# Sums of down-projection weights: from SyncE's queue to ScalarE's, from one pair of buffers to two

## The chip, the cores and the metric

The kernel runs on one core of one Trainium2 chip, in one launch. The metric is the device time of an execution in microseconds, as the median of several runs. A core has TensorE (matrix products; PE in the profile, its weight loads PEld), VectorE (DVE), ScalarE (ACT), GpSimd (POOL) and SyncE (SP). Each engine takes its instructions in the order in which they were put on it. Here SyncE issues nearly all DMAs; ScalarE and GpSimd can issue some as well, and a DMA that has to wait for a semaphore then holds up what stands behind it on the engine that issues it.

## The reference

One post-norm layer of a streaming encoder, for a prompt of 2048 tokens and for 8 sequences of 16 tokens with stored states (together 17 tiles of 128 tokens), in float32. Cut to what matters:

```
z = x @ w_in                                   # 1024 -> 2824: q,k,v,o of 4 mLSTM heads, gates, 8 q and 2 kv attention heads
hm = sigmoid(om) * head_norm(mlstm_chunkwise(qm, km * 128**-0.5, vm, logi, logf, C0, n0, m0))
ha = band_attend(rope(qa), rope(ka), va, mask, sinks)   # softmax over the window and one learned sink per head:
     # mx = max(max(s), sink);  p = exp(s - mx) / (sum(exp(s - mx)) + exp(sink - mx))
h = layer_norm(alpha * x + concat(hm, ha) @ w_out)
u = h @ w_up                                   # 1024 -> 5632
c = b_conv + causal depthwise conv of width 3 over u
a, g = split(c)
y = layer_norm(alpha * h + (silu(g) * a) @ w_down)      # 2816 -> 1024
```

## The kernel before

Every product is made of three single-pass products of a high and a low part (`hi` is the operand rounded by ScalarE, `lo` the rest, taken by VectorE: `split`, L215). The large products are done with seven half-size products in place of eight (Strassen's scheme in Winograd's form), so sums and differences of blocks of the operands are needed. For the down projection these are sums of blocks of `w_down`, and they are the subject here.

**Stages.** `i_dense` (the input projection, 4 blocks of tokens, each with 5 groups `g` of output columns and 7 products `s`), then `o_block` (the output projection, 5 blocks), then `f_ups` (up projection and convolution) and `f_downs` (down projection). While the first two run, three generators (`t_sample`, `m_chain`, `a_chain`) weave the mLSTM and the attention of finished tokens between the dense products; the class `Chains` decides by estimated costs where each step is put.

**Order.** TensorE's instructions stay in the order in which the program makes them (`manual_schedule`, L236). Those of all other engines are put in order by the framework's scheduler, for which the order of the program is a priority; an instruction that it takes to be ready can go ahead of many that stand before it.

**The products.** In input blocks 1 to 3 the products go in this order, as (g, s): (0,1) (0,7) (0,6) (0,2), then for g = 0 to 3: [(g,6) (g,7) (g,2) for g > 0], (g,5) (g+1,1) (g,3) (g,4), and (4,6) (4,7) (4,5) (4,2) (4,3) (4,4) at the end. A product is 24 matmuls (L704) into one of three banks A, B, C (`self.ib`). `i_after` (L768) moves finished banks out: copies by ScalarE (L763, L771, L779, L799), additions by VectorE (L775, L777).

**The sums.** `d_sums(k, step)` (L840) makes the two sums of pair k of weight tiles, for k = 0 to 10. Step 0 loads two tiles of 128 x 1024 (512 KB each) from `wdn` into `x` and `y` (L844, L845); step 1 is four subtractions of halves on VectorE (L850 to L853); step 2 stores both into the DRAM tensor `zt` (L855, L856), from which the down projection reads much later. `x` and `y` take the buffers `xr1` and `xr3`, one of each, so pair k + 1 can be loaded only when pair k has been stored. In input blocks 2 and 3 step 0 is written behind product s = 6 of the groups 0 to 3, step 1 behind s = 5 and step 2 behind s = 3 (for group 3: behind 6, 2 and 5), which makes k = 0 to 7. The output projection makes k = 8 to 10, one in the first half of a block (L1606).

**Who else uses these buffers.** `xr1` to `xr4` hold the four quarters of an input block (`x_load`, L534; L537 is the DMA), which `x_steps` (L539) turns into the seven operands: steps `t1` to `t4` are sums of quarters, the others split one. In the output projection `x_pair` (L884) loads its operands into the same four and splits them (L896, L897).

**The sink.** For each tile of queries `scores` (L1291, twice per tile, 32 calls in all) makes a tile `sc` of masked scores. One more column of it is filled with the sinks (L1297, GpSimd), VectorE copies the masked scores and takes their maxima (L1307), L1310 makes the bias, and `exps` (L1313) takes the exponentials with their sum, sink column included, on ScalarE.

Of the kernel before, what the change touches and what calls it, by code (L numbers as in the profile page):

```python
# [8 lines left out]
F32 = mybir.dt.float32  # L9
# [5 lines left out]
P = 128  # L15
D = 1024
# [37 lines left out]
NK2 = NFF // 2  # L54
# [150 lines left out]
class Prog:  # L205
# [381 lines left out]
    def i_dense(self):  # L587
        nc, a = self.nc, self.a
# [33 lines left out]
        for item in self.items:  # L622
# [45 lines left out]
            if g == last and b + 1 < nb:  # L668
                if s == 7:
                    self.rope_load(IBLOCKS[b + 1][2], 2)  # L670
                for x in passages[b > 0].get(s, ()):
                    if x == "load":
                        self.spare = True
                        self.x_load(b + 1, 1, 2, 3, 4)
                    else:
                        self.x_steps(b + 1, x)
            if g == last and b + 1 == nb and s in (7, 5, 2, 3):
# [1 line left out]
            with self.tc.issue_after(behind) if behind and b == 0 else nullcontext():  # L679
                self.advance()  # L680

            if b >= nb // 2 and g < last:

                steps = (6, 2, 5) if g == last - 1 else (6, 5, 3)
                if s in steps:
                    self.d_sums(sums, steps.index(s))
                    sums += s == steps[2]
        self.sums = sums
        self.logs_of(nb - 1)
        self.chains.hold = False  # L690
# [149 lines left out]
    def d_sums(self, k, step):  # L840
        nc, V = self.nc, self.nc.vector
        if step == 0:
            self.txy = x, y = [self.xp.tile([P, D], F32, name="txy", tag=f"xr{q}", bufs=1) for q in (1, 3)]
            nc.sync.dma_start(x, self.a["wdn"][k])  # L844
            nc.sync.dma_start(y, self.a["wdn"][NK2 + k])  # L845
            return
        x, y = self.txy
        if step == 1:
            l, r = slice(0, 512), slice(512, D)
            V.tensor_sub(x[:, l], x[:, r], x[:, l])  # L850
            V.tensor_sub(x[:, r], y[:, r], x[:, r])
            V.tensor_sub(y[:, r], y[:, r], x[:, l])
            V.tensor_sub(y[:, l], y[:, l], y[:, r])  # L853
            return
        nc.sync.dma_start(self.zt[0, k], x)  # L855
        nc.sync.dma_start(self.zt[1, k], y)  # L856

    def rope(self, A, t, nt):

# [411 lines left out]
    def swa(self, t):  # L1271
# [19 lines left out]
        def scores(j0):  # L1291

            sink, nsink = [x.rearrange("p (k j) -> p k j", k=2)[:, :, j0:j0 + 2] for x in (self.sink, self.nsink)]
            sc = self.work("sc", [P, 4, 2 * P + 4], bufs=2)
            mx, sm = [self.work(n, [P, 4], bufs=2) for n in ("amx", "asm")]
            w = lambda x: x.rearrange("p (k j) -> p k j", k=2)
            nc.gpsimd.tensor_copy(sc[:, :, N:N + 1].rearrange("p (k j) o -> p k (j o)", k=2), sink)  # L1297
            ps = [self.bank([P, 2, 2, P], "psc") for _ in range(2)]
            for j in range(2):
                for i, (q, k) in enumerate(((qh, self.kh), (qh, self.kl), (ql, self.kh))):  # L1300
                    for kvh in range(2):
                        rs = slice(64 * kvh, 64 * kvh + 64)
                        nc.tensor.matmul(ps[kvh][:, j, :nk], q[rs, j0 + j], k[rs, sel], start=i == 0, stop=i == 2)  # L1303
            for kvh in range(2):
                for j in range(2):
                    c = 2 * kvh + j
                    V.tensor_tensor_reduce(out=sc[:, c, :N], in0=ps[kvh][:, j, :nk].rearrange("p a b -> p (a b)"), in1=mask, scale=1.0, scalar=-3e38,  # L1307
                                           op0=ALU.add, op1=ALU.max, accum_out=mx[:, c:c + 1])

            V.scalar_tensor_tensor(w(mx), w(mx), -0.125, nsink, op0=ALU.mult, op1=ALU.min)  # L1310
            return sc, mx, sm

        def exps(sc, mx, sm):  # L1313
# [872 lines left out]
```

## Time and profile before

| | |
|---|---|
| median of 3 runs | 2317.24 us (2315.28 to 2321.0) |
| profiled execution, its own time | 2316.15 us |
| its span | 2314.3 us |
| granted TensorE clock | 0.996 |
| busy TensorE / VectorE / ScalarE / GpSimd | 99% / 78% / 55% / 12% |
| DMA, mean over the span | 273 GB/s |

A busy time is a share of the whole span, an average over stages. TensorE's number says that it hardly ever stands; where it does is read from its waits. In the rows of the profile the names on both sides of `<-` are the tile written and the tiles read, `L` is the line of the kernel, and SPq and ACTq mark DMA issues of SyncE and ScalarE.

### The profile page before, as it was taken

How to read it: one execution, taken by the hardware profiler on the slowest of the kernel's cores; microseconds unless marked ns; L12 is line 12 of the kernel's file. 1: busy time of each engine (PE TensorE's matmuls, PEld its weight loads, DVE VectorE, ACT ScalarE, POOL GpSimd, SP SyncE). 2: the span in 40 equal slices, each digit the busy share in tenths (PEclk: the TensorE clock that was granted, in tenths of full speed). 3: DMA queues.
4: the chain of work that ended last, by engine and by line, in shares of the span. 5: the costliest groups of instructions: out<-in, count | busy, mean ns of one | idle time of the engine just before them, and what ended most of it. 6: DMA issues, size and time to landing. Idle time of an engine off the chain costs nothing.

```text
span 2314.3 us, 39788 instructions
## 1 busy us (share of the span) xinstructions
PE 2281.9 (99%) x14293; PEld 2094.9 (91%) x14293; DVE 1808.1 (78%) x3075; ACT 1269.0 (55%) x2377; POOL 279.5 (12%) x509
## 2 busy tenths in 40 slices
PE   8999999999999999999999999999999999999998
PEld 8999989989877778999999999999999978888876
DVE  8777687787688888998788777678766786895987
ACT  5453466776766655555656555555555544444442
POOL 0001000000011212121002000013111200100200
PEclk9999999999999999999999999999999999999999
DMA  7888999999977757888778889978898776756743
GB/s 276 287 308 297 301 309 336 314 310 342 315 269 240 240 201 270 303 319 311 276 289 274 306 304 311 315 264 287 312 294 261 225 282 208 261 175 215 255 157 108
DMA packets 300166, 632.38 MB, mean 273 GB/s; under 512 B 47869, under 2 KB 141121, under 8 KB 299969
## 3 DMA queue, kind: packets, MB, share of 16 engines
q1 hardware_dynamic: 295296, 616.14, 77.9%
q0 software_dynamic: 3520, 10.56, 1.4%
q10 hardware_dynamic: 1152, 3.15, 0.4%
q8 instruction: 113, 1.85, 0.3%
q14 instruction: 85, 0.69, 0.1%
HBM read 458.11 MB, written 171.64 MB: 272 GB/s over the span
## 4 chain that ended last, share of the span: by engine, by line
PE 76%; DVE 5%; DMA 4%; issue 2%; ACT 1%; SPq 0%; POOL 0%; DVEq 0%; ACTq 0%; POOLq 0%
PE dps L1873 19%; PE fup L1873 19%; PE dps L704 7%; PE dps L2083 6%; PE fht L2083 6%; PE fup L2083 6%; PE dps L222 2%; PE dps L224 2%; PE dps L223 2%; PE ppo L1348 1%; PE psc L1303 1%; PE ppt L1342 1%; DVE w L218 1%; PE fht L1697 1%; DMA txy<-wdn 0%
## 5 line engine op out<-in xcount | busy, mean ns | idle before, releaser
L1873 PE MATMUL dps<-hh,uw 128*128 128x384 f32 (+1 forms) x1848 | 478.7, 328 | 2.0 <-DVE u L1904 2.0
L1873 PE MATMUL fup<-hh,uw 128*128 128x384 f32 (+1 forms) x1848 | 478.2, 328 | 1.5 <-ACT ua L1894 1.5
L1873 PEld LDWEIGHTS dps<-hh,uw 128*128 128x128 f32 x1848 | 330.5, 188 | 2.2 <-DVE u L1904 2.2
L1873 PEld LDWEIGHTS fup<-hh,uw 128*128 128x128 f32 x1848 | 330.0, 188 | 2.0 <-ACT ua L1894 1.9
L1930 DVE SCALAR_TENSOR_TENSOR cc<-u,cw,cc 128x768 f32<-128x768 f32 (+1 forms) x264 | 258.1, 978 | 64.9 <-ACT cc L1928 55.5
L1873 PE MATMUL fup<-hl,uw 128*128 128x384 f32 (+1 forms) x924 | 302.5, 327 | 1.7 <-DVE hl L218 1.7
L1873 PE MATMUL dps<-hl,uw 128*128 128x384 f32 (+1 forms) x924 | 302.8, 328 | 0.0
L704 PE MATMUL dps<-w,oh 128*128 128x256 f32 x1344 | 254.3, 284 | 0.7 <-DVE zev L777 0.7
L217 ACT CAST uw<-wraw 128x1024 fp32r<-128x1024 f32 x126 | 123.0, 979 | 223.8 <-PE dps L2083 120.1
L218 DVE TENSOR_TENSOR w<-wraw,w 128x1024 fp32r<-128x1024 f32 (+2 forms) x167 | 189.4, 1141 | 56.1 <-ACT w L217 48.9
L217 ACT CAST w<-wraw 128x1024 fp32r<-128x1024 f32 (+2 forms) x167 | 163.0, 985 | 107.3 <-PE dps L704 38.9
L704 PEld LDWEIGHTS dps<-w,oh 128*128 128x128 f32 x1344 | 210.5, 188 | 11.8 <-issue 8.1
L218 DVE TENSOR_TENSOR uw<-wraw,uw 128x1024 fp32r<-128x1024 f32 x126 | 142.4, 1131 | 65.7 <-ACT uw L217 65.5
L704 PE MATMUL dps<-w,ol 128*128 128x256 f32 x672 | 187.8, 279 | 0.0
L704 PE MATMUL dps<-oh,w 128*128 128x256 f32 x896 | 170.9, 285 | 6.6 <-ACT mr L1153 3.8
L1873 PEld LDWEIGHTS fup<-hl,uw 128*128 128x128 f32 x924 | 173.5, 188 | 2.4 <-DVE hl L218 2.3
L2083 PE MATMUL fup<-uw,fu 128*128 128x512 f32 x726 | 174.2, 396 | 0.6 <-DVE uw L218 0.6
L1873 PEld LDWEIGHTS dps<-hl,uw 128*128 128x128 f32 x924 | 173.8, 188 | 0.0
L2083 PEld LDWEIGHTS fup<-uw,fu 128*128 128x128 f32 x726 | 136.6, 188 | 34.1 <-DVE uw L218 1.1
L2083 PE MATMUL dps<-uw,fu 128*128 128x512 f32 x660 | 165.3, 396 | 1.1 <-DVE uw L218 1.1
L1928 ACT ACTIVATE cc<-u,cw 128x768 f32<-128x768 f32 (+1 forms) x132 | 132.2, 1002 | 57.8 <-DVE u L1910 28.5
L704 PEld LDWEIGHTS dps<-oh,w 128*128 128x128 f32 x896 | 142.2, 191 | 13.1 <-ACT mr L1153 4.1
(318 smaller groups left out, 4567.0 us busy)
## 6 DMA issues: line engine op xcount, KB each, us to landing
uw<-zw SPq DMA_DIRECT2D x176, 512.0 KB, 5.1
zw<-uw SPq DMA_DIRECT2D x88, 512.0 KB, 3.7
w<-zws SPq DMA_DIRECT2D x72, 512.0 KB, 6.2
wv<-wup SPq DMA_DIRECT2D x66, 512.0 KB, 5.0
wraw<-wi SPq DMA_DIRECT2D x65, 512.0 KB, 5.1
wraw<-zt SPq DMA_DIRECT2D x60, 512.0 KB, 4.3
wraw<-wdn SPq DMA_DIRECT2D x45, 512.0 KB, 4.3
wraw<-wo SPq DMA_DIRECT2D x40, 512.0 KB, 4.5
```

The costliest lines, as they stand in the source:

```text
L217: nc.scalar.copy(hi, src)
L218: nc.vector.tensor_sub(lo, src, hi.bitcast(F32))
L222: mm(out, ah, bh, start=start, stop=False)
L223: mm(out, ah, bl, start=False, stop=False)
L224: mm(out, al, bh, start=False, stop=stop)
L704: mm(o, l, r, start=s in (1, 7) and c == k == i == 0, stop=k == 3 and i == 2, skip_group_check=True)
L1303: nc.tensor.matmul(ps[kvh][:, j, :nk], q[rs, j0 + j], k[rs, sel], start=i == 0, stop=i == 2)
L1342: nc.tensor.transpose(pp[:, j * P:(j + 1) * P], scs[j // 2][:, 2 * kvh + j % 2, kt * P:(kt + 1) * P], self.ident)
L1873: mm(ps, l[:, k], r[:, k], start=s in (1, 7) and k == 0 and i == 0, stop=k == 3 and i == 2, skip_group_check=True)
L1928: S.activation(c[:, v], u[:, 2:2 + n], AF.Identity, bias=w[3], scale=w[2])
L1930: V.scalar_tensor_tensor(c[:, v], u[:, i:i + n], w[i], c[:, v], op0=ALU.mult, op1=ALU.add)
L2083: mm(ps, l[:, k, c], r[:, k], start=s in (1, 4, 7) and u == 0 and k == 0 and i == 0, stop=u == nu - 1 and k == n - 1 and i == 2, skip_grou ...
```

## The change

The loads and stores of `d_sums` are issued by ScalarE in place of SyncE. `x` and `y` take `xr1` and `xr3` for even k and `xr2` and `xr4` for odd k. In input blocks 2 and 3 step 0 is written behind product (0,1) for the first sum and behind (0,4), (1,4) and (2,4) for the next three; step 1 and step 2 stay behind 5 and 3 (for group 3: 2 and 5). `x_load` of a next block asks for the quarters in the order 1, 3, 2, 4. The sink column is copied by ScalarE, and the copy is written behind L1310. The arithmetic is the same.

```diff
@@ i_dense
                 for x in passages[b > 0].get(s, ()):
                     if x == "load":
                         self.spare = True
-                        self.x_load(b + 1, 1, 2, 3, 4)
+                        self.x_load(b + 1, 1, 3, 2, 4)
...
-            if b >= nb // 2 and g < last:
-
-                steps = (6, 2, 5) if g == last - 1 else (6, 5, 3)
-                if s in steps:
-                    self.d_sums(sums, steps.index(s))
-                    sums += s == steps[2]
+            if b >= nb // 2:
+
+                if (g, s) == (0, 1) or s == 4 and g < last - 1:
+                    self.d_sums(sums, 0)
+                    sums += 1
+                elif g < last and s in ((2, 5) if g == last - 1 else (5, 3)):
+                    self.d_sums(sums - 1, 2 if s == 3 or g == last - 1 and s == 5 else 1)
@@ d_sums
         if step == 0:
-            self.txy = x, y = [self.xp.tile([P, D], F32, name="txy", tag=f"xr{q}", bufs=1) for q in (1, 3)]
-            nc.sync.dma_start(x, self.a["wdn"][k])
-            nc.sync.dma_start(y, self.a["wdn"][NK2 + k])
+            self.txy = x, y = [self.xp.tile([P, D], F32, name="txy", tag=f"xr{q}", bufs=1) for q in ((1, 3), (2, 4))[k % 2]]
+            nc.scalar.dma_start(x, self.a["wdn"][k])
+            nc.scalar.dma_start(y, self.a["wdn"][NK2 + k])
             return
...
-        nc.sync.dma_start(self.zt[0, k], x)
-        nc.sync.dma_start(self.zt[1, k], y)
+        nc.scalar.dma_start(self.zt[0, k], x)
+        nc.scalar.dma_start(self.zt[1, k], y)
@@ scores (in swa)
-            nc.gpsimd.tensor_copy(sc[:, :, N:N + 1].rearrange("p (k j) o -> p k (j o)", k=2), sink)
...
             V.scalar_tensor_tensor(w(mx), w(mx), -0.125, nsink, op0=ALU.mult, op1=ALU.min)
+            nc.scalar.copy(sc[:, :, N:N + 1].rearrange("p (k j) o -> p k (j o)", k=2), sink)
             return sc, mx, sm
```

## The prediction, on record before the run

> **What bounds the kernel now.** I read the page first, for the engine that fills the span, then busy times in stretches for the stages that the change touches, a slice of 10 us for the clock, the waits of TensorE, and the timeline of the worst ones. The page:
>
> ```profile
> span 2314.3 us, 39788 instructions
> PE 2281.9 (99%) x14293; PEld 2094.9 (91%) x14293; DVE 1808.1 (78%) x3075; ACT 1269.0 (55%) x2377; POOL 279.5 (12%) x509
> ```
>
> TensorE is busy in all but 32.4 us. Its instruction order is fixed by hand, so only a stop of TensorE, or its clock, can change the time. The sums of the down-projection weights are made in the last two input blocks and in the output projection, which are these two stretches (length, then busy PE, PEld, DVE, ACT, POOL, clock, DMA share, GB/s); the last row is a slice out of the first:
>
> ```profile
> 255.00:560.00 305.00, 298.10 (x2537) 277.55 (x2536) 227.51 (x611) 206.41 (x510) 25.12 (x48) 0.99 0.94 316
> 560.00:840.00 280.00, 278.21 (x1765) 226.87 (x1764) 228.59 (x609) 186.15 (x480) 45.38 (x58) 1.00 0.80 269
> ...
> 330.00:340.00 10.00, 9.70 (x71) 9.57 (x72) 7.45 (x15) 8.30 (x22) 1.74 (x3) 0.84 1.03 335
> ```
>
> TensorE idles 6.9 us in the first stretch (305.00 less 298.10) and 1.8 us in the second. In the slice its clock was 0.84, which costs 10 us x 0.16 = 1.6 us. So 6.9 + 1.8 + 1.6 = 10.3 us is all that TensorE loses in the region: the most that the change could win. TensorE's longest waits in it (total, times, longest):
>
> ```profile
> PE dps L704 <- ACT mr L1153: 3.8, 1, 3.8
> PE ppt L1342 <- ACT pth L1343: 1.6, 1, 1.6
> PE pht L1176 <- DVE ql L218: 1.0, 1, 1.0
> PE ppo L1348 <- ACT pth L1343: 0.6, 1, 0.6
> ```
>
> The timeline tells what lies behind the first (start, length, engine, line; in brackets the idle time ahead of an instruction and what ended it):
>
> ```profile
> 317.33 0.32 SPq L856 DMA_DIRECT2D zt<-txy  x1
> 317.74 0.38 SPq L844 DMA_DIRECT2D txy<-wdn  x1
> ...
> 325.20 0.69 DVE L850 TENSOR_TENSOR txy<-txy 128x512 f32<-128x512 f32 x1 [3.92 <-DMA txy<-wdn]
> ...
> 328.63 0.17 ACT L1153 ACTIVATE mr<-pnum 128x2 f32<-128x2 f32 x1 [3.17 <-DVE bst L1150]
> 329.66 0.59 ACT L771 ACTIVATE zev<-dps 128x512 f32<-128x512 f32 x1
> ```
>
> I number the sums 0 to 10. With one pair of buffers the load of sum 1 goes out only when sum 0 is being stored. It lands 7.5 us later (317.74 to 325.20) and VectorE, which runs in order, stands 3.92 us before its first subtraction. ScalarE stands 3.17 us for VectorE's statistics, the eviction of a product's bank at 329.66 is queued behind that, and TensorE stands 3.8 us. Sums 6 and 7 do the same on a smaller scale:
>
> ```profile
> 505.51 0.47 SPq L856 DMA_DIRECT2D zt<-txy  x1
> 512.65 0.33 SPq L845 DMA_DIRECT2D txy<-wdn  x1
> ...
> 516.33 0.69 DVE L851 TENSOR_TENSOR txy<-txy 128x512 f32<-128x512 f32 x1 [4.37 <-DMA txy<-wdn]
> ...
> 531.74 0.56 SPq L844 DMA_DIRECT2D txy<-wdn  x1
> ...
> 539.60 0.69 DVE L850 TENSOR_TENSOR txy<-txy 128x512 f32<-128x512 f32 x1 [4.22 <-DMA zqk<-zev]
> ```
>
> Sum 6's second load went out 7.1 us behind the store that frees its buffer. The row at 539.60 names another DMA, but L850 reads only the tile loaded from 531.74 on, so I take that load for its releaser. I put the 1.0 us on L1176 down to sum 6 and the 0.6 us on L1348 to sum 7, whose lateness passes through the head norm. So VectorE's 3.92 + 4.37 + 4.22 = 12.5 us cost TensorE 3.8 + 1.0 + 0.6 = 5.4 us, 0.43 for one, and the clock's 1.6: 7.0 us hang on the loads of the sums.
>
> **The change part by part.** *Two pairs of buffers.* The other pair (xr2, xr4) lies idle meanwhile, as the next block's input loads (L537) show; xr1 and xr3 are full of sums, so the early one can only be of that pair:
>
> ```profile
> 314.24 0.47 SPq L537 DMA_DIRECT2D xr<-xq  x1
> ...
> 411.67 0.92 SPq L537 DMA_DIRECT2D xr<-xq  x1
> ...
> 420.77 0.46 SPq L537 DMA_DIRECT2D xr<-xq  x1
> ```
>
> Sums 1 and 5 need then wait for no store, and 2, 3, 6, 7 wait for the store of the sum before last. I take the three waits as gone, -7.0 us; nothing is gained if loads still land late. The rows show too that DMAs go out by readiness and not in program order: this load is written for the end of the block, 97 us further on. A load written a group sooner is therefore worth 0 by itself; sum 1's was already far ahead of its place. *What is late next:* xr2 and xr4 of the next block can no longer go early. If they go where the last loads go, at 420.77, a landing of 7.5 us as above brings them to 428; their first use (t3) is written three products behind the load, and VectorE stands if it gets there sooner. I count 0; a wait like 4.22 would cost 0.43 x 4.2 = 1.8 us. The swapped load order (1, 3, 2, 4) lets SyncE issue the free ones first: 0.
>
> *The 44 DMAs (four for each of 11 sums) leave SyncE for ScalarE.* ScalarE issues DMAs already, at 867 us:
>
> ```profile
> 867.33 0.62 ACT L896 CAST oh<-xraw 128x512 fp32r<-128x512 f32 x1 [3.52 <-DMA xraw<-zmix]
> 867.34 0.87 ACTq L1713 DMA_DIRECT2D hst<-zh  x2
> ```
>
> Two take 0.87 us, so 44 take 19 us of its sequencer, and here they run beside an instruction under way. ScalarE idles 98.6 us of the first stretch and 93.9 of the second: I take 0 for the issue alone, at most 19 us at the rate below, 1.3. The waits of these DMAs are another matter. Behind a waiting DMA stand, in order, evictions of products (L763, L771, L799), weight casts (L217) and exponentials (L1315), for all of which TensorE waits. SyncE now stands this long ahead of L844, L845, L855 and L856 (the first two and the last of 16 rows):
>
> ```profile
> SPq L855 <- DVE txy L851: 7.0, 4, 2.4
> SPq L845 <- DMA zt<-txy: 6.1, 2, 3.4
> ...
> SPq L855 <- DVE col L1026: 0.2, 1, 0.2
> ```
>
> The 16 rows come to 38.8 us. If ScalarE takes them over whole, two rates bound the price: ScalarE's idle time costs TensorE 6.9 us for 98.6 (0.07), so 2.7 us; VectorE's waits cost 0.43, so 17 us. Below nothing is open too, since SyncE, freed of these waits, could bring weights sooner: at most the 1.6 us on L1342, whose cause I have not traced. I take 2.7 us: most of what ScalarE waits for today is VectorE, and the sums' stores wait for it too, so the waits partly coincide.
>
> *Where a transfer lands sooner.* Between 860 and 885 us both queues carried 512 KB loads (KB, us to landing):
>
> ```profile
> hst<-zh ACTq DMA_DIRECT2D x4, 512.0 KB, 7.5
> ...
> wraw<-wo SPq DMA_DIRECT2D x3, 512.0 KB, 7.4
> ```
>
> No difference, so I count nothing for the queue. The Trainium skill goes further (page "DMA: Bandwidth & Descriptors", section "Issuing engines are not separate DMA queues"): all issuers share 16 DMA engines, so a second one saves issue time alone. By that rule the move to ScalarE brings no earlier data, which speaks for the third rival below.
>
> *The sink column.* One group on GpSimd:
>
> ```profile
> L1297 POOL COPY sc<-k_sink x32: 183/190/1267, 276.3 to 826.0; 128x4 f32<-128x4 f32 x32
> ```
>
> On ScalarE the nearest is the 0.17 us of L1153 above: 32 x 0.17 = 5.4 us in 550, ahead of exponentials that wait for VectorE's maxima anyway, at most 0.4 us at the rate of 0.07. GpSimd is busy 25 of 305 us and frees nothing that TensorE waits for. I take 0.
>
> Sum: 2316.15 (the profiled execution; its span is 2314.3) - 7.0 + 2.7 = 2311.85. The median, 2317.24, lies 1.1 us higher: 2312.9.
>
> **The rivals.** First, *clean removal*: the DMAs find gaps on ScalarE and hold nothing. 2317.24 - 7.0 = 2310.2, with the 1.6 us on L1342 2308.6. For it: ScalarE idles a third of the time. Against: SyncE, which computes nothing, was held 38.8 us.
>
> Second, *ScalarE held in order*, which ends slower. One wait of 3.17 us on ScalarE stood before TensorE's 3.8. If the 38.8 us pass over at 0.43: 2317.24 - 7.0 + 17 = 2327.2. From a rate of 0.18 (7.0 / 38.8) nothing is won; beyond +0.3% it is from 0.36. Against: ScalarE's average of 0.07.
>
> Third, *the pairs do not help*: DMAs go out as soon as they can, so with two pairs the sums only run closer together, the same lateness meets VectorE, and ScalarE pays 2.7: 2319.9. For it: L537's early issue, and sum 7, which waited for a load and not for a store. Against: a store before last is a whole sum older.
>
> **How the numbers follow.** 0.3% is 7 us, about what a measurement of this kernel can tell from no change. Forecast 0.36, clean 0.27, held 0.22, no help 0.15. Clean lies at the limit of 2310.3: 0.22 of it counts as faster, with 0.08 from the forecast's lower edge, where ScalarE's price falls to nothing: 0.30. Of held, 0.18 lies beyond the upper limit of 2324.2: slower 0.18. The rest, 0.52, is within. The range runs from 2308, a little past clean with the odd 1.6 us, to 2324, which leaves out most of held.
>
> **What would show it.** Right: no VectorE wait over 2 us on txy, clock 1.00 from 300 to 560 us, TensorE idle under 4 us from 255 to 560. Wrong: ScalarE standing until a store lands or L851 or L853 ends, followed by stops of TensorE on evictions; any stop over 3.8 us with the clock falling again; or VectorE still idle before L850 and L851.

## The result and the profile after

| | before | after |
|---|---|---|
| median of 22 runs each, on the same chip | 2317.05 us (2312.09 to 2324.22) | 2321.45 us (2317.78 to 2326.65) |
| profiled execution, its span | 2316.15 us, 2314.3 us | 2321.36 us, 2319.6 us |
| after / before | | 1.0024, 95% interval 1.0017 to 1.003 |

By the ratio the change costs 5.6 us (0.24% of 2317; all differences below are such ratios times 2317). That is inside the 0.3% which the prediction calls no change, and inside its range (2308 to 2324), but on the other side of zero than the forecast (2312.9). Of the predicted cases "the pairs do not help" (2319.9) comes nearest.

The page of the kernel after, span and busy engines:

```profile
span 2319.6 us, 39699 instructions
PE 2285.8 (99%) x14293; PEld 2093.9 (90%) x14293; DVE 1807.3 (78%) x3075; ACT 1271.7 (55%) x2409; POOL 273.7 (12%) x477
```

Its busy times in the two stretches that the prediction used, and in two slices (length, then busy PE, PEld, DVE, ACT, POOL, clock, DMA share, GB/s):

```profile
255.00:560.00 305.00, 295.63 (x2492) 272.79 (x2490) 222.27 (x594) 203.26 (x516) 23.91 (x32) 0.99 0.91 313
560.00:840.00 280.00, 278.41 (x1773) 226.70 (x1773) 227.30 (x616) 188.52 (x498) 37.78 (x42) 1.00 0.80 267
330.00:340.00 10.00, 9.32 (x68) 7.46 (x67) 5.55 (x12) 7.00 (x19) 1.93 (x1) 1.00 0.87 308
480.00:490.00 10.00, 7.97 (x51) 5.86 (x51) 6.33 (x13) 4.55 (x13) 3.94 (x1) 0.92 0.56 201
```

The slice from 330 us on is repaired: its clock is 1.00, where it was 0.84. But TensorE's idle time in the first stretch grew from 6.9 to 9.4 us (305.00 less 295.63), and a new slice is worse than the old one: from 480 us on TensorE works 7.97 of 10 us, at a clock of 0.92. TensorE's waits between 285 and 850 us show no single long one any more; the two largest (total, times, longest) are these, and two more are of 1.4 us:

```profile
PE pnum L1212 <- issue: 2.6, 2, 1.3
PE pht L1177 <- ACT hn L1167: 2.5, 3, 1.6
```

And the tile of the sums (lines are one higher than before: L851 to L854 are the subtractions) shows what VectorE waits for in it (total us, times):

```profile
its engine sat idle before it (us, times) until:
  DMA txy<-wdn: 17.2, 5
```

Before it was 11.0 us in 6 waits, with 4.2 us more that the profile put down to another DMA, 15.2 us together. So the waits that the change was to remove are not gone, they have moved: of the 17.2 us, 5.55 stand at 373, 5.38 at 520, 0.53 at 525, 2.99 at 536 and 2.73 at 548 us.

**Where the time went.** TensorE's 14293 instructions stand in the same order in all kernels of this case. So for each one the start in one trace can be set against the start in another. The table gives by how much a kernel's TensorE is later than the kernel before's at the same instruction (us; the instruction is named by its time in the kernel before; the difference at 285 us is taken off, since up to there the kernels hardly differ and single executions still lie up to 2.2 us apart):

| kernel | 340 | 400 | 450 | 495 | 560 | 670 | 850 |
|---|---|---|---|---|---|---|---|
| after | -2.0 | +1.0 | +1.2 | +5.4 | +5.6 | +5.3 | +5.6 |
| e1 sink column | +1.2 | +1.4 | +1.4 | +2.1 | +3.0 | +3.2 | +3.2 |
| e2 pairs | +2.4 | +5.0 | +5.1 | +4.5 | +4.2 | +2.9 | +2.9 |
| e3 queue | +2.0 | +5.4 | +5.5 | +5.7 | +4.9 | +5.9 | +6.2 |
| e4 before, tied | -1.9 | -1.5 | +6.2 | +5.6 | +3.3 | +8.2 | +10.3 |
| e5 loads swapped | -0.8 | -0.4 | -0.4 | -0.5 | -1.9 | -3.1 | -3.2 |
| e6 no subtractions | -2.1 | +0.1 | +0.1 | +0.2 | -2.1 | -3.1 | -2.8 |
| e8 after, tied | -4.0 | -2.1 | -2.0 | -1.7 | -1.5 | +1.4 | +1.9 |
| e9 pairs, tied, SyncE | -1.5 | -1.2 | +6.5 | +5.9 | +3.6 | +6.2 | +6.2 |
| e12 after, loads swapped | -3.1 | -0.5 | -0.4 | +4.9 | +4.9 | +5.2 | +5.6 |
| e13 sum 1 tied | -2.6 | -0.5 | +8.3 | +8.2 | +8.3 | +9.0 | +9.1 |
| e16 sums 0 to 3 changed | -4.3 | -1.9 | -1.8 | -1.4 | +2.3 | +0.4 | +0.4 |

Single executions scatter after 285 us too (e1's +3.2 stands beside a median only some 1 us above), so I read steps of 2 us and more. The kernel after has lost 1.8 us by 325, at two stops of 0.90 and 1.30 us that no run explains; the stop at 330, which it no longer has, brings it to 2.0 us ahead at 340. It loses 3.0 up to 400, 4.2 between 450 and 495, and little elsewhere. The loss at 480 can be followed row by row. First the power in the kernel before, then the rows of the kernel after:

```profile
480.10 1.05 POOL L1160 TENSOR_TENSOR ms<-mr,mhalf 128x4 f32<-128x4 f32 x1 [9.36 <-DVE mr L1159]
```

```profile
481.42 0.68 DVE L1110 TENSOR_TENSOR dt<-k_mcau,wi 128x512 f32<-128x512 f32 x1
481.48 3.94 POOL L1161 TENSOR_TENSOR ms<-mr,mhalf 128x4 f32<-128x4 f32 x1 [9.98 <-DVE mr L1160]
482.02 1.29 DVE L851 TENSOR_TENSOR txy<-txy 128x512 f32<-128x512 f32 x2
485.45 0.69 ACT L1167 ACTIVATE hn<-hn,ms 128x128 f32<-128x128 f32 x2 [5.83 <-POOL ms L1161]
485.91 0.62 PE L1177 MATMUL pht<-ident,hn 128*128 128x128 f32 x2 [1.59 <-ACT hn L1167]
486.97 0.62 PE L1177 MATMUL pht<-ident,hn 128*128 128x128 f32 x2 [0.44 <-ACT hn L1167]
```

The "x2" on VectorE is the thing to see. With two pairs, the loads of sums 4 and 5 go out together (465 to 471 us), both sums are ready at the same time, and their subtractions run back to back. GpSimd's power of -0.5 for the head norm runs beside them, on 128 x 4 elements. It took 1.05 us at this place before and takes 3.94 us now. A second thing has moved as well: VectorE's product in the first row starts 0.06 us ahead of the power, while before the same product started 0.57 us behind it, and there it did not lengthen the power (the last section has more cases). ScalarE's scaling waits for the power, and TensorE's transposes for ScalarE, 1.59 + 0.44 us. Then the clock falls (the same columns as above):

```profile
488.00:490.00 2.00, 2.00 (x12) 1.57 (x12) 1.82 (x3) 2.00 (x8) 0.00 (x0) 0.60 0.00 0
490.00:492.00 2.00, 2.00 (x7) 0.52 (x4) 1.92 (x5) 2.00 (x7) 0.00 (x0) 0.55 0.73 240
```

2 us x (0.40 + 0.45) = 1.7 us: the stop and the clock come to 3.7 us of the 4.2.

### The profile page after: what moved, and what is told of

It is laid out like the page before. It is cut to its first block, busy times and chain, and to the rows that moved or that the text cites. A ratio compares the mean times of both kernels' runs of the same rounds, so it can differ in the third digit from the quotient of the medians.

```text
span 2319.6 us, 39699 instructions
## 1 busy us (share of the span) xinstructions
PE 2285.8 (99%) x14293; PEld 2093.9 (90%) x14293; DVE 1807.3 (78%) x3075; ACT 1271.7 (55%) x2409; POOL 273.7 (12%) x477
## 4 chain that ended last, share of the span: by engine, by line
PE 73%; DVE 6%; DMA 5%; issue 2%; ACT 2%; POOL 0%; SPq 0%; ACTq 0%; DVEq 0%; POOLq 0%
PE dps L1874 18%; PE fup L1874 18%; PE dps L705 7%; PE dps L2084 6%; PE fht L2084 6%; PE fup L2084 6%; PE dps L222 2%; PE dps L224 2%; PE dps L223 2%; PE ppo L1349 1%; PE psc L1303 1%; DMA zf<-cc 1%; PE ppt L1343 1%; DMA w<-zws 1%; DVE cc L1931 1%
## 5 line engine op out<-in xcount | busy, mean ns | idle before, releaser
L705 PEld LDWEIGHTS dps<-w,oh 128*128 128x128 f32 x1344 | 210.6, 188 | 12.6 <-issue 8.1
L2084 PEld LDWEIGHTS dps<-uw,fu 128*128 128x128 f32 x660 | 123.9, 188 | 31.4 <-DVE uw L218 1.5
```

What stands on the lines that cost most here:

```text
L705: mm(o, l, r, start=s in (1, 7) and c == k == i == 0, stop=k == 3 and i == 2, skip_group_check=True)
L2084: mm(ps, l[:, k, c], r[:, k], start=s in (1, 4, 7) and u == 0 and k == 0 and i == 0, stop=u == nu - 1 and k == n - 1 and i == 2, skip_grou ...
```

## The experiments

All were run against the kernel before on the same chip; each line gives the median, the ratio to before and its 95% interval. The names of the theories are those of the expectations. A: the subtractions stand in VectorE's order ahead of their loads' landing, and TensorE pays for VectorE's waits and clumps. B: ScalarE is held by the DMAs it issues. C: any change deals the fixed order of VectorE, ScalarE and SyncE out anew, and a new order has stops of its own.

**e1, the sink column alone**

```diff
-            nc.gpsimd.tensor_copy(sc[:, :, N:N + 1].rearrange("p (k j) o -> p k (j o)", k=2), sink)
...
             V.scalar_tensor_tensor(w(mx), w(mx), -0.125, nsink, op0=ALU.mult, op1=ALU.min)
+            nc.scalar.copy(sc[:, :, N:N + 1].rearrange("p (k j) o -> p k (j o)", k=2), sink)
```

> The kernel before with one edit: the sink column copied by ScalarE. Theory A (the subtractions of the sums stand in VectorE's order ahead of the time at which their loads land, whatever buffers and queue; TensorE pays for VectorE's waits and for subtractions in a clump): within 1 us of before, as 32 copies of 0.2 us lie on ScalarE's idle time. Theory B (ScalarE, in order, is held by what is added to it): +0.4 us by the prediction's lower rate, +3 us by its upper one (6 us x 0.43). If the copy is what makes the changed kernel slower: +5 us.

2318.43 us, 1.0005 (0.9995 to 1.0016): no difference shown. The prediction's 0 lies inside the interval, which reaches from 1.2 us faster to 3.7 us slower.

**e2, two pairs (and the order of the next block's loads) alone, on SyncE**

```diff
-                        self.x_load(b + 1, 1, 2, 3, 4)
+                        self.x_load(b + 1, 1, 3, 2, 4)
...
-            self.txy = x, y = [self.xp.tile([P, D], F32, name="txy", tag=f"xr{q}", bufs=1) for q in (1, 3)]
+            self.txy = x, y = [self.xp.tile([P, D], F32, name="txy", tag=f"xr{q}", bufs=1) for q in ((1, 3), (2, 4))[k % 2]]
```

> The kernel before with one edit: two pairs of buffers in turn and the load order 1, 3, 2, 4; the DMAs stay on SyncE and where they are written. Theory A: the pairs do not settle where the subtractions stand, so VectorE still waits for some load by more than 2 us, and the time is within 4 us of before on either side. Theory B: all of the 7 us that hang on the one pair come back, 2310, and no wait of VectorE on the loads is over 2 us.

2320.48 us, 1.002 (1.001 to 1.003): slower by 4.6 us, where theory B wanted the gain. VectorE's waits for the sums' loads are 12.6 us in 5, little shorter than the 15.2 us before, and the stop at 330 stays (3.4 us).

**e3, ScalarE's queue alone, one pair**

```diff
-            nc.sync.dma_start(x, self.a["wdn"][k])
+            nc.scalar.dma_start(x, self.a["wdn"][k])
...
```

The other load and both stores are changed alike.

> The kernel before with one edit: loads and stores of the sums issued by ScalarE, one pair of buffers. Theory A: ScalarE's waits are mostly under idle time, so within 3 us of before; VectorE's waits on the loads stay at 10 to 20 us in all. Theory B: ScalarE takes over SyncE's 38.8 us of waits, and the kernel is slower by 5 us or more, with stops of TensorE on evictions behind ScalarE's DMAs.

2321.40 us, 1.0024 (1.0015 to 1.0033): slower by 5.6 us. VectorE's waits for these loads rise to 24.1 us in 9. The stop at 330 moves to a later instruction: TensorE stands 2.80 us ahead of the one that starts at 334.55 us in the kernel before.

So neither half carries a gain, and each costs about as much as the whole change. That the loads are written a group sooner, the third part of the change, was not run by itself, nor was the new order of the next block's loads.

**e4, the kernel before with the subtractions tied later**

```diff
-                    self.d_sums(sums, steps.index(s))
+                    with self.tc.issue_after(self.last_add) if s == steps[1] else nullcontext():
+                        self.d_sums(sums, steps.index(s))
```

(`last_add` is the last addition of the product behind which step 1 is written; the tie holds in VectorE's order.)

> The kernel before with one edit: the four subtractions of a sum in the input blocks may not go ahead of the last addition of a product that the program writes ahead of them; loads, stores, queue and buffers as before. Theory A: the loads have landed by then, no wait of VectorE on the loads over 0.5 us in the input blocks, the stop of 3.85 us near 326 and the drop of the clock behind it are gone, 2310 to 2312 (-5 to -7 us). Theory B: as ScalarE and SyncE are unchanged, what it gains is the same 5 to 7 us; it tells A from B only by failing: if the time stays within 2 us of before, VectorE's waits on the loads are not what TensorE pays for.

2326.88 us, 1.0048 (1.0032 to 1.0064): 11 us slower, where theory A expected a gain of some 6. The stop at 330 did go (table: -1.9 at 340), and the waits fell to 7.2 us in 3. But 7.7 us are lost between 400 and 450, and more after 560. Theory A in its simple form falls; what happens at 433 is followed under e13.

**e5, the two loads swapped**

```diff
-            nc.sync.dma_start(x, self.a["wdn"][k])
             nc.sync.dma_start(y, self.a["wdn"][NK2 + k])
+            nc.sync.dma_start(x, self.a["wdn"][k])
```

> The kernel before, with the two loads of a sum written in the other order (y, then x); buffers, queue, places and arithmetic stay, and TensorE's order too, while the order of VectorE's work changes in many places. Theory A (the cost lies in VectorE's waits for these loads): the same loads land at about the same time, so within 1.5 us of the kernel before (2315.5 to 2318.5 us). Theory C (any change to this work deals VectorE's and ScalarE's order out again, and a new order has stops of its own of 1 to 4 us at places that have nothing to do with the sums): 2318.5 to 2323 us or, less likely, 2311 to 2314 us, with single stops of over 1 us that the kernel before does not have.

2315.29 us, 0.9987 (0.9973 to 1.0002): perhaps 3 us faster, not shown. The trace tells where: VectorE waits as much as before (10.9 us in 6), but GpSimd's power of -0.5 at 652 us no longer runs on beside one of the sums' subtractions and a second weight split. Before, and with the loads swapped:

```profile
652.26 3.63 POOL L1160 TENSOR_TENSOR ms<-mr,mhalf 128x4 f32<-128x4 f32 x1 [6.92 <-DVE mr L1159]
655.92 1.28 ACT L1166 ACTIVATE hn<-hn,ms 128x128 f32<-128x128 f32 x4 [4.09 <-POOL ms L1160]
```

```profile
651.42 1.89 POOL L1160 TENSOR_TENSOR ms<-mr,mhalf 128x4 f32<-128x4 f32 x1 [6.62 <-ACT w L217]
```

ScalarE's scaling stands 4.09 us for the power, and behind it stands the copy for which TensorE waits 1.6 us on L1342 at 657. The prediction left that stop untraced; it is gone here (-1.8 us at that instruction).

**e6, no subtractions at all**

```diff
-            V.tensor_sub(x[:, l], x[:, r], x[:, l])
-            V.tensor_sub(x[:, r], y[:, r], x[:, r])
-            V.tensor_sub(y[:, r], y[:, r], x[:, l])
-            V.tensor_sub(y[:, l], y[:, l], y[:, r])
+            pass
```

> The kernel before without the four subtractions of each sum (loads and stores stay, so the output is not the reference's): VectorE is rid of 44 x 0.67 us = 29.5 us and of all 15 us of waits for these loads. Theory A: TensorE gets back the stops behind those waits, about 5.4 us and 1.6 us of clock, 2308 to 2311 us, and no new stops. Theory C: the order is dealt out again here too, so less than half of it comes back or none, 2312 to 2320 us, with new stops of over 1 us.

2311.93 us, 0.9978 (0.9966 to 0.9991): faster by 5.1 us, 2.1 to 7.9 by the interval. This kernel leaves out the subtractions, so its output is not the layer's. All that the sums cost on VectorE, 29.5 us of work and 15 us of waits, comes out at less than the 7.0 us that the forecast took for three of the waits, though the interval does not exclude 7.0. The table shows one reason: the 2.1 us won at 340 are gone at 400, with no sums in the way. The next thing due there is a row of the mLSTM that goes through DRAM and back. First the kernel before, then this one:

```profile
348.11 0.59 POOL L1078 DMA_DIRECT2D zM<-r_M  x1 [11.50 <-DVE r_M L1077]
353.71 0.57 POOL L1080 DMA_DIRECT2D wi<-zM  x1 [5.01 <-DMA wraw<-wi]
359.46 0.66 DVE L1109 TENSOR_TENSOR dt<-k_mcau,wi 128x512 f32<-128x512 f32 x1
```

```profile
343.97 0.59 POOL L1075 DMA_DIRECT2D zM<-r_M  x1 [11.86 <-DVE r_M L1074]
350.01 0.57 POOL L1077 DMA_DIRECT2D wi<-zM  x1 [5.45 <-DMA zM<-r_M]
357.50 0.69 DVE L1106 TENSOR_TENSOR dt<-k_mcau,wi 128x512 f32<-128x512 f32 x1 [2.63 <-DMA wi<-zM]
```

The row sets out 4.1 us sooner and VectorE can use it only 2.0 us sooner, after a wait of 2.63 us for its return. This execution is 2.0 us ahead at 285 us already, so counted as in the table the row is usable no sooner at all. ScalarE's steps behind it come no sooner either, and TensorE stops for 1.51 us at 365.70. Before, the stop at 330 covered that trip. In e8 and e16 TensorE stops at the same instruction (0.75 and 1.26 us), but VectorE does not wait for the row there; what holds ScalarE in those two I have not followed.

**e7, the subtractions on GpSimd**

```diff
-            V.tensor_sub(x[:, l], x[:, r], x[:, l])
+            nc.gpsimd.tensor_sub(x[:, l], x[:, r], x[:, l])
...
```

The other three subtractions move alike.

> The kernel before with the sums' subtractions on GpSimd in place of VectorE. VectorE neither works nor waits for the sums. Theory A (VectorE's waits were the cost): the stop at 330 goes, 2309 to 2313 us, unless GpSimd takes its place: a subtraction there should take about 1.3 us (the rows of its 128x512 work), four of them 5.2 us, and its waits for the loads stand ahead of its powers of -0.5 (17 of them), on which ScalarE's scaling of hn and then TensorE's transposes wait; if two or three of the 17 are held by 5 us, 2317 to 2325 us, and the stops name ms<-mr. Theory C: new stops that name neither.

2341.92 us, 1.0103 (1.0084 to 1.0122): 24 us slower, beyond the rival's 2317 to 2325. The waits stand on GpSimd now, whose own few steps are waited for: from 285 to 850 us ScalarE stands 47.2 us for the powers (30.2 in the kernel before), and TensorE's longest stop is 5.8 us at 530. The first subtraction of each sum:

```profile
L850 POOL TENSOR_TENSOR txy<-txy 128x512 f32<-128x512 f32 x11 | 23.0, 2089 | 71.5 <-DMA txy<-wdn 60.4 <-DVE mr L1159 7.6 <-ACT oh L896 3.6
```

This subtraction takes 2.1 us in the mean (0.69 on VectorE), and GpSimd stands 71.5 us in all ahead of the first of each four.

**e8, the kernel after with the subtractions tied as in e4**

```diff
-                    self.d_sums(sums - 1, 2 if s == 3 or g == last - 1 and s == 5 else 1)
+                    step = 2 if s == 3 or g == last - 1 and s == 5 else 1
+                    with self.tc.issue_after(self.last_add) if step == 1 else nullcontext():
+                        self.d_sums(sums - 1, step)
```

> The kernel after, with the subtractions tied in VectorE's order behind the last addition of the product they are written at, so that sums 4 and 5 no longer run back to back at 482. Theory A: that stop of 4.3 us goes and VectorE's waits for these loads fall from 17.2 us to under 8 us; since there are two pairs, the next block's loads are not held as they were when the kernel before was tied so; 2312 to 2317 us. Theory C: the waits fall, but new stops come at other places, 2318 us or more.

2317.55 us, 1.0000 (0.9989 to 1.0011): level with the kernel before, so tying gives back what the change cost. VectorE waits for no load of the sums at all, and the power at 480 no longer runs beside two sums:

```profile
479.99 1.53 POOL L1163 TENSOR_TENSOR ms<-mr,mhalf 128x4 f32<-128x4 f32 x1 [9.94 <-DVE mr L1162]
482.67 1.03 PE L1179 MATMUL pht<-ident,hn 128*128 128x128 f32 x4
```

TensorE does not wait for the transposes at 482.67. Yet a kernel without a single one of these waits is no faster than the one with 15 us of them. It is 2.0 us ahead up to 450 and loses that again: 1.7 us at 549, and 2.3 us at 642, where ScalarE's order now has a weight's cast ahead of the exponentials and stands for its load (the profile names another DMA; by the times I take the load issued at 633.71 for its releaser):

```profile
633.71 0.51 SPq L461 DMA_DIRECT2D wraw<-wo  x1
638.19 1.05 ACT L217 CAST w<-wraw 128x1024 fp32r<-128x1024 f32 x1 [5.70 <-DMA zkv<-zev]
645.28 0.47 PE L1214 MATMUL pnum<-v,dt 128*128 128x129 f32 x2 [2.17 <-DVE asm L1321]
```

**e9, two pairs and tied subtractions on SyncE**

The edits are those of e2 and e4 together. Beside e8 it differs by the queue and the sink column, as the expectation says, and by a third thing that the expectation leaves out: the loads are written where the kernel before has them, not a group sooner.

> The kernel before with two pairs of buffers (and the order of the next block's loads that goes with them) and the subtractions tied behind the last addition of the product they are written at; DMAs stay on SyncE, the sink column on GpSimd. It differs from the run tied so before it by the queue and the sink column alone. Theory B (ScalarE held by the DMAs it issues costs time): faster than that run by 2.5 us or more, under 2315.5 us. Theory A: both are free of VectorE's waits for these loads, so about the same, 2316 to 2319 us; and the stop of 4 us at 433 of the kernel before tied so (one pair, held until the subtractions are done, and the next block's loads behind it) is gone. Theory C: another deal, 2312 to 2322 us; the stop at 642 (a weight's cast on ScalarE put ahead of the landing of its load) may go.

2323.32 us, 1.0033 (1.0021 to 1.0045): 7.6 us slower. Theory B expected the opposite of what came: with late subtractions the kernel that issues from ScalarE is the faster one, by these 7.6 us (the sink column had made no difference in e1). SyncE's issues and TensorE here:

```profile
411.04 0.46 SPq L856 DMA_DIRECT2D zt<-txy  x1
414.32 0.32 SPq L857 DMA_DIRECT2D zt<-txy  x1
...
423.23 1.11 SPq L537 DMA_DIRECT2D xr<-xq  x2
427.20 0.95 SPq L537 DMA_DIRECT2D xr<-xq  x2
...
436.73 0.36 PE L705 MATMUL dps<-w,oh 128*128 128x256 f32 x1 [2.06 <-DMA w<-zws]
438.56 0.50 PE L705 MATMUL dps<-w,oh 128*128 128x256 f32 x2 [1.35 <-DMA w<-zws]
```

SyncE takes the stores of the late sum 3 in its turn, and the four loads of the next block go out behind them in 5 us. They used to be spread (in the kernel before 314 to 421 us, in e8 396 to 421). The kept weights (`w<-zws`, split in an earlier block and read back from DRAM) go out behind those, the first of them at 428.25 us (421.34 in the kernel before, 421.47 in e8), and TensorE stops. So two pairs by themselves do not keep the next block's loads free, as the expectation of e8 had it. What does is either the queue or the place of the loads: in e8 SyncE has no stores to stand for, but sum 3's second load also goes out at 364.58 us, and here at 404.52. No run parts the two.

**e10, e8 with the loads swapped**

> The kernel after, tied in VectorE's order as before, with the two loads of a sum in the other order (y, then x). VectorE's order is the same as without the swap, ScalarE's differs in some 40 places. Theory A: 2316 to 2319 us, as without the swap. Theory C: moves by 1.5 us or more to either side, by stops that follow ScalarE's order.

2316.97 us, 1.0003 (0.9992 to 1.0013): as e8. The swap that seemed to win 3 us in e5 wins nothing here.

**e11, the kernel before with the two stores swapped**

> The kernel before with the two stores of a sum in the other order (y, then x). VectorE's order changes in some 15 places only, TensorE's not at all. Theory A: within 1.5 us of the kernel before. Theory C: also near it, since little is dealt out again (the swap of the loads, with 230 lines of VectorE's order changed, moved it by -3 us): 2315 to 2319 us, and TensorE's stops at the same places.

2316.31 us, 1.0005 (0.9991 to 1.0018): no difference, as both theories had it.

**e12, the kernel after with the loads swapped**

> The kernel after with the two loads of a sum in the other order (y, then x), nothing tied. Theory A: the subtractions still stand ahead of their loads, VectorE's waits stay near 17 us: 2319 to 2323 us. Theory C: the order is dealt out again; the clump of sums 4 and 5 at 482 with the 3.9 us power of -0.5 on GpSimd may go (then 2316 to 2318 us) or stay, and other stops come; 2314 to 2326 us.

2321.65 us, 1.0025 (1.0014 to 1.0035): as the kernel after. This one is worth a look beside e8, since it halves VectorE's waits and leaves the clump:

```profile
  DMA txy<-wdn: 8.7, 3
```

```profile
481.36 3.94 POOL L1161 TENSOR_TENSOR ms<-mr,mhalf 128x4 f32<-128x4 f32 x1 [10.15 <-DVE mr L1160]
```

With 8.5 us of waits less the time is the same (table: +5.3 between 450 and 495). The waits that are gone all stood from 520 us on: 11.6 us in the kernel after, 2.4 here, and from 495 to 560 TensorE loses 0.2 us there and nothing here. So the clump at 482 is paid for, and those waits are not. The wait at 373 is still there (6.27 us), so this run says nothing of the 3.0 us lost before 400.

**e13, only sum 1 of the kernel before tied**

```diff
+                    with self.tc.issue_after(self.last_add) if s == steps[1] and sums in (1,) else nullcontext():
                         self.d_sums(sums, steps.index(s))
```

> The kernel before with the subtractions of sum 1 alone tied behind the last addition of the product they are written at: one pair, SyncE's queue, all else untouched. This takes away the wait of VectorE before the stop at 330 and nothing else on purpose. Theory A (that wait cost 3.8 us of stop and 1.6 us of half clock): 2310.5 to 2313.5 us, no stop at 330. Theory C (what is gained there is given back by the order dealt out anew after it): the stop at 330 goes too, but 2314 to 2320 us, with new stops of over 1 us between 335 and 660.

2322.72 us, 1.0036 (1.0024 to 1.0049): 8.3 us slower (5.6 to 11.4). The one wait behind the stop at 330 is taken away, but by running sum 1 later (its first subtraction moves from 325 to 353 us), not by loading it sooner as the change meant to. The stop goes (-2.6 at 340) and 8.8 us are lost between 400 and 450:

```profile
420.47 0.47 SPq L856 DMA_DIRECT2D zt<-txy  x1
...
426.59 1.14 SPq L537 DMA_DIRECT2D xr<-xq  x2
427.78 1.12 SPq L483 DMA_DIRECT2D w<-zws  x1
...
434.32 0.36 PE L705 MATMUL dps<-w,oh 128*128 128x256 f32 x1 [2.98 <-DMA w<-zws]
438.25 0.79 PE L705 MATMUL dps<-w,oh 128*128 128x256 f32 x2 [3.46 <-DMA w<-zws]
```

Sum 1 later makes 2 and 3 later, since they share one pair. Sum 3 is stored at 420 us (403.74 before), and the next block's last two loads, those of `xr1` and `xr3`, which wait for that, go out at 426.59 and right behind, in place of 411.67 and 420.77. In SyncE's order the kept weights stand right behind the last of these loads. In the kernel before they went out here:

```profile
421.34 1.16 SPq L483 DMA_DIRECT2D w<-zws  x2
```

The two loads of this row go out at 427.78 and 431.56 us in e13, 6.4 and 9.4 us later, and TensorE stands for just these. The trip itself is no longer: the first takes 6.4 us to land, 7.0 before. Nor are the 16 DMA engines any busier than in the same stretch before (the figure ahead of the last; first the kernel before, then this one):

```profile
430.00:440.00 10.00, 10.00 (x83) 9.02 (x82) 5.63 (x9) 7.50 (x16) 2.56 (x4) 1.00 1.02 348
```

```profile
430.00:440.00 10.00, 3.56 (x21) 3.05 (x20) 3.77 (x5) 4.48 (x11) 1.11 (x2) 0.75 1.03 361
```

The same two loads go out 6 to 13 us late in e4, e9, e14 and e15, which all lose at 433, and at most 0.7 us off in e8 and e16, which have no stop at 330 and lose nothing there. So what e13 shows is the price of a late sum on one pair and one queue, and not that the stop at 330 was needed.

**e14 and e15: sums 1, 6 and 7 tied; the same with the loads swapped**

> The kernel before with the subtractions of sums 1, 6 and 7 tied so: the three waits of VectorE that the forecast counted are gone, with one pair on SyncE's queue; the next block's loads, which sum 3 held up where all were tied, are not touched. Theory A: the 7.0 us of the forecast's sum come back, 2309 to 2312 us. Theory C: 2313 to 2321 us, with the stops at 330, 518 and 550 gone and others in their place.

> As the run before it, with the loads of a sum in the other order (y, then x). Theory A: as without the swap, 2309 to 2312 us. Theory C: no sum of the two single results (the swap alone gave -3 us, unclear); anywhere from 2310 to 2321 us.

2323.24 us, 1.0038 (1.0026 to 1.0051), and 2325.38 us, 1.0043 (1.0029 to 1.0056). Theory A's 2309 to 2312 is far off. In e14 the stops of sums 6 and 7 go as well (-1.2 and -0.7 us at 518 and 550 us), and the loss at 433 (8.1 us between 400 and 450) outweighs all three.

**e16, the change for sums 0 to 3 alone, tied; the last block as before**

```diff
-            self.txy = x, y = [self.xp.tile([P, D], F32, name="txy", tag=f"xr{q}", bufs=1) for q in (1, 3)]
+            self.txy = x, y = [self.xp.tile([P, D], F32, name="txy", tag=f"xr{q}", bufs=1) for q in ((1, 3), (2, 4))[k in (1, 3)]]
+            q = nc.scalar if k < 4 else nc.sync
-            nc.sync.dma_start(x, self.a["wdn"][k])
+            q.dma_start(x, self.a["wdn"][k])
...
-            if b >= nb // 2 and g < last:
+            if b == nb // 2:
...
+            if b > nb // 2 and g < last:
```

Under the first condition stand the steps of the kernel after, tied as in e8; under the second those of the kernel before. The sink column and the order of the next block's loads are those of the kernel after.

> The change for sums 0 to 3 alone (two pairs, ScalarE's queue, loads a group sooner, subtractions tied behind their product's last addition, next block's loads in the order 1, 3, 2, 4; sink column on ScalarE), sums 4 to 7 of the last block and all later ones as in the kernel before. Theory A': the stop at 330 goes (3.4 us), none comes at 433, and the stops at 549 and 642 (1.7 and 2.5 us), which came with the sums of the last block, do not come: 2312 to 2315 us. Theory C: the order of the last block is dealt out again as well, so new stops there: 2316 to 2321 us.

2315.73 us, 0.9994 (0.998 to 1.0007): no difference shown. Up to 495 it does what theory A' said: 1.4 us ahead, no stop at 433. In the last block, whose sums are written as before, one stop takes it back:

```profile
540.10 0.69 DVE L859 TENSOR_TENSOR txy<-txy 128x512 f32<-128x512 f32 x1 [5.72 <-DMA zqk<-zev]
551.38 1.80 PE L1358 MATMUL ppo<-pth,kva 128*64 128x512 f32 x4 [2.14 <-ACT pth L1353]
```

It is sum 7's old wait, 5.72 in place of 4.22 us; I take TensorE's 2.14 us (0.6 before) to follow from it.

**e17, e16 with the loads of sums 4 and later swapped**

> As e16, with the loads of a sum swapped (y, then x) for sums 4 and later alone, which in the kernel before took 2.8 us off the last block. If gains add up: 2.0 us from before 450 and 2.8 us from the last block, 2311 to 2314 us. Theory C: the last block falls anew and the gain is not kept: 2315 to 2320 us, with a stop of over 1.5 us between 480 and 700.

2315.84 us, 0.9999 (0.9986 to 1.0012). Its profiled execution is 2.7 us ahead of the kernel before's at 850, as the sum of the gains would have it, but the twelve runs have the median of e16. Nothing that I ran is shown to be faster than the kernel before with the sums in it.

## Why the prediction was wrong, step by step

**"I take the three waits as gone, -7.0": the step that failed, three times over.** First, they were not gone: VectorE waited 17.2 us in place of 15.2. The prediction's reason, that the pair is free in time, held for the buffers, but not for the order: the framework puts a subtraction into VectorE's order where it takes it to be ready, and sum 3's first one ran at 355.69 us, its second load went out at 366.44, and VectorE stood 5.55 us ahead of its second:

```profile
366.44 0.35 ACTq L846 DMA_DIRECT2D txy<-wdn  x1
373.60 0.69 DVE L852 TENSOR_TENSOR txy<-txy 128x512 f32<-128x512 f32 x1 [5.55 <-DMA txy<-wdn]
```

The sentence "nothing is gained if loads still land late" had named this and given it no price. Second, the price was too high. The stop of 3.8 us and its clock, 5.4 us together, were real, and the stop is gone in all kernels that spared the wait; but in e8 and e16, where nothing is lost at 433, TensorE is 4.0 and 4.3 us ahead at 340 and 2.0 and 1.8 us at 450. In e6, without any subtraction, the 2.1 us won are gone at 400, because the trip of a row through DRAM comes back no sooner. The prediction had asked what is late next only of the buffers xr2 and xr4, not of all that comes due behind the stop. Third, the rate of 0.43, total stop by total wait, does not carry over: e12 had 8.5 us of waits less and the same time. The waits of sums 6 and 7 were priced nearer: where they are spared (e14), their two stops go as well, 1.9 us for the 1.6 that were counted.

**What was not in the sum: the clump.** Two pairs make two sums ready at once, and the two together ran against GpSimd's power: 4.2 us between 450 and 495, shown by e12 (clump, +5.3 there) against e8 (no clump, +0.3) and by the rows. Of the 3.0 us lost between 340 and 400 the cause stays open: e8, without a wait on the sums' loads, loses 1.9 us there too. The third rival said "the sums only run closer together" and priced that at nothing.

**ScalarE's 44 DMAs, +2.7:** here the mechanism was right and the size stays open. The 38.8 us of SyncE's waits did not pass over whole; by the trace the 44 DMAs held ScalarE 15.7 us together (the time from the end of its instruction before to the issue), 5.3 of them at 374, where the store waits for the subtraction that itself waits for its load. By the rate of 0.07 that would be 1.1 us. What it costs depends on the order of the rest: alone it was 5.6 us slower (e3), while among the kernels with late subtractions the one that issues from ScalarE is 7.6 us faster (e8 against e9, which also differ in where the loads are written). The prediction saw only the price of a second queue and not a use that it may have, that the next block's loads and the kept weights do not stand behind the sums' stores. The Trainium skill (page "DMA: Bandwidth & Descriptors", section "Issuing engines are not separate DMA queues") says that another issuing engine saves only the time to initiate a DMA. In e9 the loss lies elsewhere, in what stands behind other DMAs on its issuer: the kept weights go out 6.9 us late, and TensorE stands 3.4 us for them.

**The sink column, 0:** no difference shown, so nothing against it (e1).

**The next block's loads no longer early, 0:** right in the kernel after, whose loads go out at 373 and 381 us, sooner than the last ones before (411 and 421). They did not go where the prediction put them, at 420.77. Where the last of them do go late, TensorE loses 8.8 us (e13), not the 1.8 that was named, and through the kept weights behind them, not through t3.

**The signs to look for:** "VectorE still idle before L850 and L851" was the one that came true, beside a stop with the clock falling, of 2.0 us and not of over 3.8. "Clock 1.00 from 300 to 560" failed at 488 to 492.

**Theory C** is not the whole story either. Of the edits that change no work and no resource, the swap of the stores (e11) and of the loads (e10 beside e8, e12 beside the kernel after) moved nothing, and that in e5 perhaps 3 us. The larger losses have a cause that the rows name: the loads at 433 (e4, e9, e13 to e15), the clump (after, e12), GpSimd (e7). What e2 and e3 lose before 400 I have not followed to its end. Not settled either is why the stops at 549 and 642 in e8 and at 551 in e16 come: they follow from ScalarE's and VectorE's order, and no run took one of them away by itself. Nor did a run test by itself the stop of about 1.3 us in the kernel after near 390, for which the profile names only "issue": the instruction reads `dt`, and VectorE's row that writes it (389.93 us, 0.68 long) ends 0.1 us before.

## What to carry to other kernels

Before a stop is counted as a gain, ask of every transfer and round trip behind it, and not only of the buffers that the change touches, whether it would have been in time without the stop; here half of what was won at 340 was lost again by 450 (e8, e16). A wait of an engine is worth what its removal gives in a run, not its length by a rate. Running work later to spare a wait is another change than bringing its data sooner: e13 spared the wait so and paid for it 80 us further on, at loads that stood behind the late work. And where instructions of an in-order engine are placed by readiness, more buffers move work together as well as forward: look at what runs beside it when two pieces come at once.

## What the runs showed of the hardware

GpSimd's power of -0.5 on 128 x 4 elements is held by a run of VectorE instructions with two inputs in SBUF that is under way as it starts. With no such run under way it takes 1.03 to 1.05 us, even if VectorE begins a weight split of 1.22 us 0.06 us behind it (the kernel before at 430.50). With one under way it ends some 0.9 us behind the run's end: 1.89 us beside one split (e5 at 651.42), 2.49 beside a split and one 0.69 us product (the kernel before at 787.65), 3.94 beside such a product and four subtractions of 0.69 that follow it without a pause. A pause of 0.03 us between two subtractions is enough to let it through: 1.36 us at 334.30 in the kernel before. A subtraction with one operand in PSUM does not lengthen it: 1.89 us again at 755 us there, beside a split and 0.68 us of such a one. Of the 34 powers of the kernels before and after one does not fit, at 397 in the kernel after: two products of 128 x 256 follow a split without a pause and do not lengthen it. The Trainium skill has a sentence that fits (page "VectorE: DVE Perf Modes", section "Two Vector instructions with no wait between them"): it calls the second SBUF read interface, through which VectorE reads its second SBUF input, shared with GpSimd. The rows agree, PSUM operands included; no run took the second SBUF input away by itself.

The clock stood at 0.50 for 3.4 us, from 488.4 us on (0.60 and 0.55 in the two stretches above), behind two stops of 1.59 and 0.44 us with 0.6 us of work between them. Single stops of 3.85 us (the kernel before at 330), 2.17 us (e8 at 645) and 2.14 us (e16 at 551) were each followed by 3.4 us at 0.50 too; one of 1.65 us (the kernel before at 657) was not.
